# Head denominators as extra columns of the value matmuls, and a new order of casts, splits and SiLUs around the four heads, in a two-layer decoder trunk

## The chip, the cores and the metric

The kernel runs on one core of one Trainium2 chip. The metric is the device time of one execution in microseconds (us). The kernel before takes 823.21 us, the median of three runs (823.09 to 824.32).

A core has these engines, each with its own instruction queue: TensorE (PE, matmuls, with its weight loads shown apart as PEld), VectorE (DVE), ScalarE (ACT), GpSimd (POOL) and SyncE (SP, which issues the loads here).

## The reference

The reference takes 256 tokens of width 1024 through two layers. Layer 0 mixes tokens with a gated MLP, layer 1 with an mLSTM block; each layer goes on with a SwiGLU channel mixer and a gated per-layer embedding, and each residual sum goes through a layer norm. What the change touches is the mLSTM's cell and its output projection. For 256 tokens in two chunks of 128 and a state that starts at zero, a head's cell comes down to this:

```python
s   = (q @ k.T) * d ** -0.5 * exp(dmat - m_t)        # causal, per head; dmat from the gates
num = s @ v                                          # 512 columns of values
den = sum(s, axis=-1)
h   = num / maximum(abs(den), exp(-m_t))
h   = layer_norm(h, norm_g) + skip * xc              # over the head's 512 columns
y   = (h * silu(z)) @ w_out                          # four heads side by side: 2048 features
x   = layer_norm(ALPHA * x + y, ...)
```

The four heads have 512 columns each. `den` is the sum of a row of scores, so it is also `s @ 1`.

## The kernel before, in words

**Precision.** Each matmul of fp32 data is made of three: a value is split into a high and a low part, and high·high, high·low and low·high are added up in PSUM. `split(hi, lo, src)` (lines 150 to 152) is two instructions: a cast on ScalarE writes `hi`, and a subtraction writes `lo`, on VectorE if nothing is said, on GpSimd with `sub=pool`.

**Weights.** All weights stream from DRAM in a fixed list (`weight_plan`). SP loads one piece of 128x1024 (512 KB) at a time into one of four buffers `raw`, at most `LOAD_AHEAD` = 8 pieces ahead of the piece in use. `ahead` (from line 166) also casts and splits up to `CAST_AHEAD` = 4 pieces ahead into one of six buffers `w`: a ScalarE cast and a VectorE subtraction of 128x1024. A `raw` buffer comes free when its subtraction has read it, and only then can SP issue the load that takes its place. The pieces of the output projection are called `mo`, 0 to 15; `pj` and `f` are the first pieces of the channel mixer behind it.

**Order.** A scheduler at build time sets each engine's order from the order in which the code is written and from its own estimates. `issue_after(ops)` holds the instructions in it behind given ones in that order; `behind["cast"]` is such a list for the weights' casts. The engines then run their queues in order and wait on semaphores.

**The mLSTM stage.** It makes the values of each head: `vn[h]` holds 512 high and 512 low columns of each of two token halves. It makes the scores and the gate factors, and per head the weighted scores `sc` (line 910), which are split into `phi` (ScalarE) and `plo` (GpSimd). Then come the four heads. `pv_block(h)` (lines 921 to 963) does this:

- nine matmuls of 512 columns into two PSUM banks `num`, one per token half (lines 930, 931, 934), then six of two columns against a tile of ones into a third bank `pd` (lines 938, 939), which gives the denominators;
- VectorE: the denominator `dn` (944 to 948), statistics of each `num` bank (952, 953), and the scale `rs` and the bias `nb` of the normalization (956, 958, 960), with a power on GpSimd between (957); below, "nb of head h" is the last of these, which the change's text calls the head's norm;
- ScalarE: two instructions of 128x512 that read `num` and write the normalized head `hn` (line 962), after which the banks are free.

Between the heads TensorE makes the last four pieces of `z` (features 12 to 15, bank `zps`, 24 matmuls of 256 columns each), and ScalarE's `z_act` (line 744) writes their SiLU. Four earlier pieces get theirs together in one instruction of 128x1024 (line 916). `h_block(h)` (lines 967 to 981) transposes the head on TensorE (972, bank `tp`) and makes four features on VectorE: `y` = scale and skip (976), `y` times SiLU (977), and a split of `y` into `h`.

**The output projection** multiplies features 0 to 15 with `mo` 0 to 15 into four banks `acc`, two for each token half (lines 238 to 240). PSUM has two pools of four banks, A and B. Heads 0 to 3 take their `num` banks from A in turn, then `acc` does: the first token half's two banks are those that head 2 had, the second half's those of head 3. The first three features are done for the first token half (18 matmuls) and then for the second (18 matmuls), so that the second half's banks are asked for later; features 3 to 15 follow, with the transposes of heads 2 and 3 between them. Behind the projection stands the layer norm of each token half (lines 333 to 342) and the transposes of its result (line 324), on which the channel mixer's matmuls wait.

Of the kernel before, what the change touches and what calls it, by code (L numbers as in the profile page):

```python
# [132 lines left out]
def trunk(ctx, tc, a, out):  # L133
# [35 lines left out]
    def ahead(loads, casts):  # L169
        while at["load"] < min(len(plan), at["use"] + loads):  # L170
            ap = plan[at["load"]][1]
            n = ap.shape[-1]

            t = tl("row" if plan[at["load"]][0] == ("mo", 8) else "raw", [P, n], name="raw")
            for c in HALF if at["load"] < 3 else [slice(0, n)]:
                at["dma"] = sp.dma_start(t[:, c], ap[:, c])
            raws[at["load"]] = t
            at["load"] += 1
        while at["cast"] < min(len(plan), at["use"] + casts):
            i = at["cast"]  # L180
            key, raw = plan[i][0], raws.pop(i)
            n = raw.shape[-1]
            if key in WIDE:
                t = tl("b8", [P, 2, D], F32R, "w")
            else:


                first = ASIDE if stationary(key) and not paired(key) else 0
                step = D + ASIDE if paired(key) else D
                t = tl("w", [P, 2 * D + P], F32R, "w")[:, first:first + 2 * step]  # L190
                t = t.rearrange("p (i n) -> p i n", i=2)[:, :, :D]
            with issue_after(behind["cast"]):
                if key[0] == "bdv":

                    t = t.rearrange("p i n -> p (i n)")[:, :4 * 2 * GW].rearrange("p (j i n) -> p j i n", j=4, i=2)
                    split(t[:, :, 0, :P], t[:, :, 1, :P], raw.rearrange("p (j n) -> p j n", j=4))
                    f = 4 * key[1]
                    pool.tensor_copy(t[:, :, :, P:], wx[:, f:f + 4, :].rearrange("p j (i n) -> p j i n", i=2))
                for c in () if key[0] == "bdv" else HALF if i < 3 else [slice(0, n)]:
                    split(t[:, 0, c], t[:, 1, c], raw[:, c])  # L200
            wt[i] = t
            at["cast"] += 1
# [492 lines left out]
    def mlstm(embed1):  # L695
# [30 lines left out]
        vn = [tl("b8", [P, 2, 2, 512], F32R, "vn") for _ in range(NH)]  # L726
# [16 lines left out]
        def z_act(f, ps):  # L743
            act.activation(sz[f // 8][:, f % 8, :], ps, AF.Silu)

        def z_copy(f, ps):
            act.copy(sz[f // 8][:, f % 8, :], ps)
# [27 lines left out]
        def qv_block(f):  # L775
# [13 lines left out]
            o = tl("cf", [P, 3 * P], name="vsum")[:, :2 * GW].rearrange("p (t n) -> p t n", t=2)  # L789
# [6 lines left out]
            split(vn[h][:, 0, :, c], vn[h][:, 1, :, c], o[:, :, :P], sub=pool)  # L796
# [55 lines left out]
        with tc.manual_schedule(engines={mybir.EngineType.Activation}):  # L852
# [62 lines left out]
            z_copy(*z)  # L915
            act.activation(sz[1][:, 0:4, :], sz[1][:, 0:4, :], AF.Silu)
# [6 lines left out]
        def pv_block(h):  # L923
            hi, lo = ph[h]
            pd = bank("B", [P, 2, 2], "pd")
            num = [bank("A", [P, 512], "num") for _ in range(2)]

            for t, blocks in enumerate(BLOCKS):
                for i, (s, c) in enumerate(blocks):
                    pe.matmul(num[t], hi[:, c], vn[h][:, 0, s, :], start=i == 0, stop=False)  # L930
                    pe.matmul(num[t], hi[:, c], vn[h][:, 1, s, :], start=False, stop=False)
            for t, blocks in enumerate(BLOCKS):
                for i, (s, c) in enumerate(blocks):
                    pe.matmul(num[t], lo[:, c], vn[h][:, 0, s, :], start=False, stop=i == len(blocks) - 1)

            for t, (s, c) in DEN:
                first, end = s == 0, s == t
                pe.matmul(pd[:, t, :], hi[:, c], ones_r[:, :2], start=first, stop=False)
                pe.matmul(pd[:, t, :], lo[:, c], ones_r[:, :2], start=False, stop=end)
# [4 lines left out]
            dve.scalar_tensor_tensor(dn, pd[:, :, 0], -1.0, cols[:, 2:4, h], ALU.mult, ALU.max)  # L944
            dve.tensor_tensor(dn, dn, pd[:, :, 0], ALU.max)
# [3 lines left out]
            st = tl("c", [P, 2, 6], name="hst")  # L949
            mv = tl("c", [P, 2, 2], name="hmv")  # L950
            for t in range(2):
                end = dve.bn_stats(st[:, t, :], num[t])
                dve.bn_aggr(mv[:, t, :], st[:, t, :])
# [6 lines left out]
            dve.scalar_tensor_tensor(nb, mv[:, :, 0], -1.0, rs, ALU.mult, ALU.mult)  # L960
            for t in range(2):
                act.activation(o[:, t, :], num[t], AF.Identity, bias=nb[:, t:t + 1], scale=rs[:, t:t + 1])
            return (end,)

        hs = {}

        def h_block(h):
            for j in range(2):
# [4 lines left out]
                for i in range(2):  # L973
                    f = 4 * h + 2 * j + i
                    y = tl("s", [P, S], name="y")
                    dve.scalar_tensor_tensor(y, tp[:, i, :], par[:, f, 6:7], a1[f // 8][:, f % 8, :], ALU.mult, ALU.add)
                    dve.tensor_tensor(y, y, sz[f // 8][:, f % 8, :], ALU.mult)
                    hs[f] = tl("h", [P, 2, S], F32R, "h")
                    split(hs[f][:, 0, :], hs[f][:, 1, :], y)

        for h in range(NH):
            if h == NH - 1:
                ahead(LOAD_AHEAD, 4)
            end = pv_block(h)
            z_act(*z_mm(12 + h))
            if h == NH - 2:
                h_block(0)
        acc = Down(NI)
        begin = []
        for h in range(NH):  # L990
            if h == 2:
                load_p(1)
            if h + 1 < NH:
                h_block(h + 1)
            for f in range(4 * h, 4 * h + 4):
                if f == 1:

                    behind["cast"] = end
                block = (f, hs.pop(f), weight("mo", f, casts=1 if f >= NI - 2 else None))
                if f < 3:  # L1000

                    begin.append(block)
                    for t in range(2) if f == 2 else ():
                        for b, h2, w in begin:
                            acc.mm(b, t, h2, w)
                else:
# [99 lines left out]
```

## Time and profile before

| | value |
|---|---|
| time, median of 3 runs | 823.21 us (823.09 to 824.32) |
| time of the profiled execution | 823.71 us |
| its span, first to last instruction | 822.0 us |
| TensorE busy | 816.2 us, 99% of the span, 4546 matmuls |
| VectorE busy | 616.9 us, 75% |
| ScalarE busy | 471.8 us, 57% |
| GpSimd busy | 152.1 us, 19% |
| granted TensorE clock | 0.999 of full speed |
| the four heads (first to last matmul against values) | 535.1 to 555 us of the span |
| the output projection, with its layer norm | 559.0 to 613 us |

The profiled execution took 1.7 us more than its span and 0.5 us more than the median. Busy time of a matmul is longer than its place in the queue, since matmuls overlap: what one costs is read from start to start. Rows of the timeline give the start, the length, the engine, the line, the operation and its output and inputs, and, in brackets, how long the engine stood idle before it and what released it.

### The profile page before, as it was taken

What the parts mean: (1) busy time and instruction counts of PE and PEld (TensorE: products, weight loads), DVE (VectorE), ACT (ScalarE), POOL (GpSimd) and SP (SyncE); (2) the same over time, 40 slices, a digit from 0 to 9 for tenths busy, and PEclk for the clock granted to TensorE, in tenths of its full rate; (3) what the DMA queues carried; (4) which work ended last, traced back from release to release, by engine and by line L of the source; (5) the groups of instructions that cost most, each with busy time, mean ns of one, the idle gap of its engine ahead of it and who ended that gap; (6) DMA issues with size and microseconds to landing.
All of it is one profiled execution on the core that took longest, in us unless ns stands there. A gap on an engine that the chain in (4) does not pass through costs nothing.

```text
span 822.0 us, 12471 instructions
## 1 busy us (share of the span) xinstructions
PE 816.2 (99%) x4546; PEld 709.1 (86%) x4546; DVE 616.9 (75%) x985; ACT 471.8 (57%) x824; POOL 152.1 (19%) x209
## 2 busy tenths in 40 slices
PE   9999999999999999999999999999999999999997
PEld 6888888888888888888889999998888888888886
DVE  6667998678966567587878998889896566776674
ACT  6556666565554455465256788776544455665522
POOL 1120643343000000700001677430000000000000
PEclk9999999999999999999999999999999999999999
DMA  8885447558176668667144345453635667886501
GB/s 300 306 306 180 153 156 228 179 182 274 42 258 195 216 217 283 202 228 246 43 151 154 125 164 165 152 199 129 207 126 193 198 206 234 274 256 209 180 1 52
DMA packets 44998, 155.54 MB, mean 189 GB/s; under 512 B 5256, under 2 KB 6024, under 8 KB 44936
## 3 DMA queue, kind: packets, MB, share of 16 engines
q1 hardware_dynamic: 44504, 154.21, 57.2%
q8 instruction: 36, 0.59, 0.3%
q10 hardware_dynamic: 432, 0.52, 0.2%
q14 instruction: 26, 0.21, 0.1%
HBM read 153.67 MB, written 1.05 MB: 188 GB/s over the span
## 4 chain that ended last, share of the span: by engine, by line
PE 98%; DMA 1%; DVE 0%; ACTq 0%; ACT 0%; issue 0%; DVEq 0%
PE acc L238 9%; PE acc L239 9%; PE acc L240 9%; PE pu L258 9%; PE pg L258 9%; PE ups L258 5%; PE pg L262 5%; PE pu L262 5%; PE ups L262 3%; PE vps L240 2%; PE vps L238 2%; PE vps L239 2%; PE xmps L243 2%; PE xmps L244 2%; PE xmps L245 2%; PE gate L287 2%
## 5 line engine op out<-in xcount | busy, mean ns | idle before, releaser
L152 DVE TENSOR_TENSOR w<-raw,w 128x1024 fp32r<-128x1024 f32 (+1 forms) x275 | 333.1, 1219 | 70.1 <-ACT w L152 69.2
L152 ACT CAST w<-raw 128x1024 fp32r<-128x1024 f32 (+1 forms) x275 | 284.9, 1046 | 104.2 <-PE acc L240 23.4
L238 PE MATMUL acc<-w,h 128*128 128x512 f32 x336 | 133.0, 396 | 0.0
L239 PE MATMUL acc<-w,h 128*128 128x512 f32 x336 | 131.3, 391 | 0.0
L240 PE MATMUL acc<-w,h 128*128 128x512 f32 x336 | 131.0, 390 | 0.0
L258 PE MATMUL pu<-xs,w 128*128 128x512 f32 x320 | 79.4, 390 | 0.0
L258 PE MATMUL pg<-xs,w 128*128 128x512 f32 x320 | 79.3, 390 | 0.0
L240 PEld LDWEIGHTS acc<-w,h 128*128 128x128 f32 x336 | 63.1, 188 | 13.8
L238 PEld LDWEIGHTS acc<-w,h 128*128 128x128 f32 x336 | 63.1, 188 | 11.3
L239 PEld LDWEIGHTS acc<-w,h 128*128 128x128 f32 x336 | 63.2, 188 | 11.1
L258 PEld LDWEIGHTS pg<-xs,w 128*128 128x128 f32 x320 | 59.9, 188 | 12.4
L258 PEld LDWEIGHTS pu<-xs,w 128*128 128x128 f32 x320 | 59.8, 188 | 12.3
L269 ACT COPY s<-pg 128x256 f32<-128x256 f32 x40 | 14.9, 372 | 92.1 <-PE pg L262 92.1
L317 POOL TENSOR_TENSOR rs<-ve,mhalf 128x1 f32<-128x1 f32 x8 | 7.6, 954 | 296.7 <-DVE ve L316 251.8
L270 DVE TENSOR_TENSOR s<-s,pg 128x256 f32<-128x256 f32 x40 | 16.8, 420 | 60.7 <-ACT s L269 60.6
L258 PE MATMUL ups<-xs,w 128*128 128x512 f32 x192 | 47.9, 392 | 0.0
L262 PEld LDWEIGHTS pg<-xs,w 128*128 128x128 f32 x320 | 43.2, 188 | 3.4
L262 PE MATMUL pg<-xs,w 128*128 128x256 f32 x320 | 43.9, 280 | 0.0
L262 PE MATMUL pu<-xs,w 128*128 128x256 f32 x320 | 43.8, 279 | 0.0
L258 PEld LDWEIGHTS ups<-xs,w 128*128 128x128 f32 x192 | 35.7, 188 | 7.2
L262 PEld LDWEIGHTS pu<-xs,w 128*128 128x128 f32 x320 | 40.6, 188 | 0.3
L243 PE MATMUL xmps<-xs,w 128*128 128x256 f32 x128 | 36.3, 284 | 0.0
(251 smaller groups left out, 1587.0 us busy)
## 6 DMA issues: line engine op xcount, KB each, us to landing
raw<-in_ffn_d SPq DMA_DIRECT2D x44, 512.0 KB, 4.3
raw<-in_ffn_g SPq DMA_DIRECT2D x40, 512.0 KB, 4.3
raw<-in_ffn_u SPq DMA_DIRECT2D x40, 512.0 KB, 4.1
raw<-in_gm_u SPq DMA_DIRECT2D x24, 512.0 KB, 3.3
raw<-in_gm_wo SPq DMA_DIRECT2D x24, 512.0 KB, 3.3
raw<-in_gm_v SPq DMA_DIRECT2D x21, 512.0 KB, 5.2
raw<-in_ple_gate SPq DMA_DIRECT2D x16, 512.0 KB, 4.5
raw<-in_ml_z SPq DMA_DIRECT2D x16, 512.0 KB, 3.4
```

The costliest lines, as they stand in the source:

```text
L152: return dve.tensor_copy(hi, src) if fast else act.copy(hi, src), sub.tensor_tensor(lo, src, hi.bitcast(F32), ALU.subtract)
L238: pe.matmul(ps, lh, w[:, 0, c], start=start, stop=False)
L239: pe.matmul(ps, ll, w[:, 0, c], start=False, stop=False)
L240: pe.matmul(ps, lh, w[:, 1, c], start=False, stop=stop)
L243: pe.matmul(ps, w[:, 0, c], h, start=start, stop=False)
L244: pe.matmul(ps, w[:, 0, c], l, start=False, stop=False)
L245: pe.matmul(ps, w[:, 1, c], h, start=False, stop=stop)
L258: pe.matmul(ps, w[:, 0, k * P:(k + 1) * P], xs[:, k], start=k == 0, stop=False)
L262: pe.matmul(ps[:, 0], w[:, 1, k * P:(k + 1) * P], xh[:, k, :], start=False, stop=k == KD - 1)
L269: act.copy(o, ps[:, 1])
L270: dve.tensor_tensor(o, o, ps[:, 0], ALU.add)
L287: pe.matmul(ps, xl[:, k, TOK[t]], w[:, 0, c], start=False, stop=k == KD - 1)
```

## The change

- **Values.** `vn[h]` becomes one tile with two views: `vh`, 512 high columns and two columns of ones for each token half, and `vl`, 512 low columns. GpSimd copies the ones once per head. The sum `vsum` moves to another group of buffers.
- **`pv_block`.** The two-column matmuls and the bank `pd` go. A head now takes three banks `num`: `low` from pool A has columns 0 to 255 of both token halves, `top` from A and from B has columns 256 to 511 of one half each and two columns more, the first of which is the denominator. Nine matmuls of 512 columns become eighteen of 256 or 258. The first two operations of `dn` are done per token half (128x1, two of each), the statistics in four instructions of 256 columns instead of two of 512, the normalization in four ScalarE instructions of 128x256 instead of two of 128x512.
- **Casts.** `behind` can hold a list for a single piece. The casts of `mo` 0 to 3 are each held behind an operation on ScalarE and one on VectorE: `mo` 0 behind nb of head 0, `mo` 1 behind nb of head 1, `mo` 2 behind the `y` of feature 1, `mo` 3 behind nb of head 3; later casts stand behind nb of head 3, as before.
- **SiLUs.** The SiLUs of `z` 12 and 13 stand behind the `hn` of head 0, the one of 128x1024 behind the `hn` of head 1 (it stood before that of head 0).
- **Head 0's last feature**, 3, is held back behind nb of head 3, and head 1's transposes move from before the projection's first token half to between the two halves.

On TensorE, the end of head 0's matmuls against the values (`vn` values, `phi` and `plo` scores). Before:

```order
L930 MATMUL num<-vn,phi 128x512
L931 MATMUL num<-vn,phi 128x512
L934 MATMUL num<-vn,plo 128x512 x3
L938 MATMUL pd<-ones_r,phi 128x2
L939 MATMUL pd<-ones_r,plo 128x2
```

Now:

```order
L940 MATMUL num<-vn,phi 128x256
L941 MATMUL num<-vn,phi 128x258
L943 MATMUL num<-vn,phi 128x256 x2
L947 MATMUL num<-vn,plo 128x256
L948 MATMUL num<-vn,plo 128x258
```

The matmuls into `pd` (six per head) are gone; each matmul of 512 columns stands there as two.

On VectorE, head 0's denominators and normalization (`w` from `raw` is the low part of a projection weight, `sc` the weighted scores of a later head). Before:

```order
L910 SCALAR_TENSOR_TENSOR sc<-sc,e 128x384
L944 SCALAR_TENSOR_TENSOR dn<-pd,cols 128x2
L152 TENSOR_TENSOR w<-raw,w 128x1024
L945 TENSOR_TENSOR dn<-dn,pd 128x2
L910 SCALAR_TENSOR_TENSOR sc<-sc,e 128x384
L946 RECIPROCAL dn<-dn 128x2
L948 TENSOR_TENSOR dn_5717<-dn 128x2
L952 BN_STATS hst<-num 128x6 x2
L953 BN_AGGR hmv<-hst 128x2 x2
L956 TENSOR_SCALAR hrs<-hmv,dn_5717 128x1 x2
L958 TENSOR_TENSOR hrs<-hrs,dn 128x2
L960 SCALAR_TENSOR_TENSOR nb<-hmv,hrs 128x2
```

Now:

```order
L956 RECIPROCAL dn<-dn 128x2
L958 TENSOR_TENSOR dn_5725<-dn 128x2
L963 BN_STATS hst<-num 128x6 x3
L916 SCALAR_TENSOR_TENSOR sc<-sc,e 128x384
L964 BN_AGGR hmv<-hst 128x2
L963 BN_STATS hst<-num 128x6
L967 TENSOR_SCALAR hrs<-hmv,dn_5725 128x1
L964 BN_AGGR hmv<-hst 128x2
L967 TENSOR_SCALAR hrs<-hmv,dn_5725 128x1
L969 TENSOR_TENSOR hrs<-hrs,dn 128x2
L971 SCALAR_TENSOR_TENSOR nb<-hmv,hrs 128x2
L152 TENSOR_TENSOR w<-raw,w 128x1024
```

The low parts of the first two projection weights stood before nb of head 0; the first of them now follows it, and there is one behind nb of head 1, one between nb of heads 2 and 3, and the fourth behind nb of head 3.

On ScalarE, the same place (`sz` the gate, `hn` the normalized head). Before:

```order
L744 ACT_TABLE_LOAD
L744 ACTIVATE sz<-zps 128x256
L916 ACTIVATE sz<-sz 128x1024
L962 ACTIVATE hn<-num,nb,hrs 128x512 x2
L152 CAST w<-raw 128x1024
```

Now:

```order
L152 CAST w<-raw 128x1024
L975 ACTIVATE hn<-num,nb,hrs 128x256 x4
L748 ACT_TABLE_LOAD
L748 ACTIVATE sz<-zps 128x256 x2
L152 CAST w<-raw 128x1024
L975 ACTIVATE hn<-num,nb,hrs 128x256 x4
L1015 ACTIVATE sz<-sz 128x1024
```

The table load and the SiLUs moved from ahead of head 0's normalization to behind it, the SiLU of 128x1024 to behind that of head 1.

```diff
-            with issue_after(behind["cast"]):
+            with issue_after(behind.get(key, behind["cast"])):
...
-        vn = [tl("b8", [P, 2, 2, 512], F32R, "vn") for _ in range(NH)]
+        vn = [tl("b8", [P, 2 * D + P], F32R, "vn") for _ in range(NH)]
+        vh = [v[:, :1028].rearrange("p (s n) -> p s n", n=514) for v in vn]
+        vl = [v[:, D + P:].rearrange("p (s n) -> p s n", n=512) for v in vn]
...
-            split(vn[h][:, 0, :, c], vn[h][:, 1, :, c], o[:, :, :P], sub=pool)
+            split(vh[h][:, :, c], vl[h][:, :, c], o[:, :, :P], sub=pool)
+            if j == 3:
+                pool.tensor_copy(vh[h][:, :, 512:], ones_r[:, :4].rearrange("p (s n) -> p s n", s=2))
...
-            z_copy(*z)
-            act.activation(sz[1][:, 0:4, :], sz[1][:, 0:4, :], AF.Silu)
+            behind["hn", -1] = z_copy(*z)
...
-            pd = bank("B", [P, 2, 2], "pd")
-            num = [bank("A", [P, 512], "num") for _ in range(2)]
+            halves = slice(0, 256), slice(256, 512)
+            low = bank("A", [P, 2, 256], "num")
+            top = [bank(w, [P, 258], "num") for w in "AB"]
+
+            den = [n[:, 256:257] for n in top]
+            num = [(low[:, t, :], top[t][:, :256]) for t in range(2)]
 
             for t, blocks in enumerate(BLOCKS):
                 for i, (s, c) in enumerate(blocks):
-                    pe.matmul(num[t], hi[:, c], vn[h][:, 0, s, :], start=i == 0, stop=False)
-                    pe.matmul(num[t], hi[:, c], vn[h][:, 1, s, :], start=False, stop=False)
+
+                    pe.matmul(low[:, t, :], hi[:, c], vh[h][:, s, :256], start=t == i == 0, stop=False)
+                    pe.matmul(top[t], hi[:, c], vh[h][:, s, 256:], start=i == 0, stop=False)
+                    for n, half in zip(num[t], halves):
+                        pe.matmul(n, hi[:, c], vl[h][:, s, half], start=False, stop=False)
             for t, blocks in enumerate(BLOCKS):
                 for i, (s, c) in enumerate(blocks):
-                    pe.matmul(num[t], lo[:, c], vn[h][:, 0, s, :], start=False, stop=i == len(blocks) - 1)
-
-            for t, (s, c) in DEN:
-                first, end = s == 0, s == t
-                pe.matmul(pd[:, t, :], hi[:, c], ones_r[:, :2], start=first, stop=False)
-                pe.matmul(pd[:, t, :], lo[:, c], ones_r[:, :2], start=False, stop=end)
+                    end = i == len(blocks) - 1
+                    pe.matmul(low[:, t, :], lo[:, c], vh[h][:, s, :256], start=False, stop=end and t == 1)
+                    pe.matmul(top[t], lo[:, c], vh[h][:, s, 256:], start=False, stop=end)
...
-            dve.scalar_tensor_tensor(dn, pd[:, :, 0], -1.0, cols[:, 2:4, h], ALU.mult, ALU.max)
-            dve.tensor_tensor(dn, dn, pd[:, :, 0], ALU.max)
+            for t in range(2):
+                dve.scalar_tensor_tensor(dn[:, t:t + 1], den[t], -1.0, cols[:, 2 + t, h:h + 1], ALU.mult, ALU.max)
+                dve.tensor_tensor(dn[:, t:t + 1], dn[:, t:t + 1], den[t], ALU.max)
...
-                end = dve.bn_stats(st[:, t, :], num[t])
-                dve.bn_aggr(mv[:, t, :], st[:, t, :])
+                for i in range(2):
+                    dve.bn_stats(st[:, t, i, :], num[t][i])
+                dve.bn_aggr(mv[:, t, :], st[:, t])
...
-            dve.scalar_tensor_tensor(nb, mv[:, :, 0], -1.0, rs, ALU.mult, ALU.mult)
+            end = dve.scalar_tensor_tensor(nb, mv[:, :, 0], -1.0, rs, ALU.mult, ALU.mult)
+            behind["norm", h] = behind["norm"] = end,
             for t in range(2):
-                act.activation(o[:, t, :], num[t], AF.Identity, bias=nb[:, t:t + 1], scale=rs[:, t:t + 1])
-            return (end,)
+                for n, half in zip(num[t], halves):
+                    behind["hn", h] = act.activation(o[:, t, half], n, AF.Identity, bias=nb[:, t:t + 1], scale=rs[:, t:t + 1])
...
+                    if f == 3:
+                        held.append((f, tp[:, i, :]))
+                    else:
+                        h_feature(f, tp[:, i, :])
...
             if h == NH - 1:
+                behind["mo", 0] = behind["hn", -1], behind["norm", 0][0]
+                behind["mo", 1] = z13, behind["norm", 1][0]
+                behind["mo", 2] = behind["hn", 1], behind["y", 1]
                 ahead(LOAD_AHEAD, 4)
-            end = pv_block(h)
-            z_act(*z_mm(12 + h))
-            if h == NH - 2:
+            pv_block(h)
+            z = z_mm(12 + h)
+            with issue_after((behind["hn", 0],) if h == 0 else ()):
+                z13 = z_act(*z) if h < 2 else z13
+            if h == 2:
+                with issue_after((behind["hn", 1],)):
+                    act.activation(sz[1][:, 0:4, :], sz[1][:, 0:4, :], AF.Silu)
+            if h >= 2:
+                z_act(*z)
+            if h == 2:
                 h_block(0)
+        behind["mo", 3] = behind["hn", 2], behind["norm"][0]
+        with issue_after(behind["norm"]):
+            h_feature(*held.pop())
         acc = Down(NI)
         begin = []
         for h in range(NH):
             if h == 2:
                 load_p(1)
-            if h + 1 < NH:
+            if h == 0:
+                ahead(LOAD_AHEAD, 4)
+            if 0 < h < NH - 1:
                 h_block(h + 1)
             for f in range(4 * h, 4 * h + 4):
                 if f == 1:
-
-                    behind["cast"] = end
+                    behind["cast"] = behind["norm"]
...
                     for t in range(2) if f == 2 else ():
                         for b, h2, w in begin:
                             acc.mm(b, t, h2, w)
+                        if t == 0:
+                            with issue_after(behind["norm"]):
+                                h_block(1)
```

More of the change, by code (lines that the diff above doesn't have):

```diff
@@ L743, in z_act @@
         def z_act(f, ps):
-            act.activation(sz[f // 8][:, f % 8, :], ps, AF.Silu)
+            return act.activation(sz[f // 8][:, f % 8, :], ps, AF.Silu)
         def z_copy(f, ps):
-            act.copy(sz[f // 8][:, f % 8, :], ps)
+            return act.copy(sz[f // 8][:, f % 8, :], ps)
         xms, qs = {}, {}
@@ L788, in qv_block @@
             c = slice(j * P, (j + 1) * P)
-            o = tl("cf", [P, 3 * P], name="vsum")[:, :2 * GW].rearrange("p (t n) -> p t n", t=2)
+            o = tl("m2", [P, 2 * GW], name="vsum").rearrange("p (t n) -> p t n", t=2)
             for t in range(2):
@@ L948, in pv_block @@
             dve.tensor_tensor(dn2, dn, dn, ALU.mult)
-            st = tl("c", [P, 2, 6], name="hst")
+            st = tl("c", [P, 2, 2, 6], name="hst")
             mv = tl("c", [P, 2, 2], name="hmv")
             for t in range(2):
-                end = dve.bn_stats(st[:, t, :], num[t])
-                dve.bn_aggr(mv[:, t, :], st[:, t, :])
+                for i in range(2):
+                    dve.bn_stats(st[:, t, i, :], num[t][i])
+                dve.bn_aggr(mv[:, t, :], st[:, t])
             rs = tl("c", [P, 2], name="hrs")
@@ L959, in pv_block, with h_feature @@
             nb = tl("c", [P, 2], name="nb")
-            dve.scalar_tensor_tensor(nb, mv[:, :, 0], -1.0, rs, ALU.mult, ALU.mult)
+            end = dve.scalar_tensor_tensor(nb, mv[:, :, 0], -1.0, rs, ALU.mult, ALU.mult)
+            behind["norm", h] = behind["norm"] = end,
             for t in range(2):
-                act.activation(o[:, t, :], num[t], AF.Identity, bias=nb[:, t:t + 1], scale=rs[:, t:t + 1])
-            return (end,)
+                for n, half in zip(num[t], halves):
+                    behind["hn", h] = act.activation(o[:, t, half], n, AF.Identity, bias=nb[:, t:t + 1], scale=rs[:, t:t + 1])
         hs = {}
+        def h_feature(f, tp):
+            y = tl("s", [P, S], name="y")
+            behind["y", f] = dve.scalar_tensor_tensor(y, tp, par[:, f, 6:7], a1[f // 8][:, f % 8, :], ALU.mult, ALU.add)
+            dve.tensor_tensor(y, y, sz[f // 8][:, f % 8, :], ALU.mult)
+            hs[f] = tl("h", [P, 2, S], F32R, "h")
+            split(hs[f][:, 0, :], hs[f][:, 1, :], y)
+        held = []
         def h_block(h):
@@ L974, in h_block @@
                     f = 4 * h + 2 * j + i
[L975 to L979, printed above, removed]
+                    if f == 3:
+                        held.append((f, tp[:, i, :]))
+                    else:
+                        h_feature(f, tp[:, i, :])
         for h in range(NH):
             if h == NH - 1:
+                behind["mo", 0] = behind["hn", -1], behind["norm", 0][0]
+                behind["mo", 1] = z13, behind["norm", 1][0]
+                behind["mo", 2] = behind["hn", 1], behind["y", 1]
                 ahead(LOAD_AHEAD, 4)
-            end = pv_block(h)
-            z_act(*z_mm(12 + h))
-            if h == NH - 2:
+            pv_block(h)
[8 more added lines that the diff above has]
+            if h == 2:
                 h_block(0)
+        behind["mo", 3] = behind["hn", 2], behind["norm"][0]
+        with issue_after(behind["norm"]):
+            h_feature(*held.pop())
         acc = Down(NI)
```

## The prediction

> **What bounds the kernel now.** I read the page first, then TensorE's waits, then the timelines around the four heads and around the layer norm behind the projection. The page's busy row, the chain that ended last, and all the waits of TensorE over the whole program:
>
> ```profile
> PE 816.2 (99%) x4546; PEld 709.1 (86%) x4546; DVE 616.9 (75%) x985; ACT 471.8 (57%) x824; POOL 152.1 (19%) x209
> PE 98%; DMA 1%; DVE 0%; ACTq 0%; ACT 0%; issue 0%; DVEq 0%
> PE warm L355 <- PEq L1096: 0.8, 1, 0.8
> PE vps L419 <- ACT xs L375: 0.5, 1, 0.5
> ```
>
> TensorE sets the end and waits nowhere in the heads or in the projection. A microsecond less on TensorE is therefore worth up to a microsecond, but only where nothing else comes to bind in its place; a microsecond on the other engines is worth nothing until it makes TensorE wait.
>
> **What the change takes from TensorE.** Head 0's matmuls against the values, its two-column matmuls, and the `z` piece behind them (start, length):
>
> ```profile
> 535.10 0.39 PE L930 MATMUL num<-vn,phi 128*128 128x512 f32 x1
> ...
> 537.18 0.17 PE L938 MATMUL pd<-ones_r,phi 128*128 128x2 f32 x1
> ...
> 537.76 0.36 PE L243 MATMUL zps<-xs,w 128*128 128x256 f32 x1
> 537.96 0.28 PE L244 MATMUL zps<-xs,w 128*128 128x256 f32 x1
> 538.08 0.28 PE L245 MATMUL zps<-xs,w 128*128 128x256 f32 x1
> ```
>
> The six small matmuls take 537.76 - 537.18 = 0.58 us, and the first matmul behind them holds the queue for 0.20 instead of 0.12: 0.66 per head. The nine of 512 columns take 537.18 - 535.10 = 2.08; eighteen of 256 at 0.12 or a little less take 2.1 to 2.16, some 0.04 more. Left are 0.62 per head and 2.5 us for four: TensorE's ceiling is 823.2 - 2.5 = 820.7 us. Nothing else in the change takes anything from TensorE; the moved transposes stay eight, in another place.
>
> **Where that gain must pass.** From the projection's second token half on, TensorE's work is the same matmuls as before. The end moves as that start moves, unless a later wait is new. The start needs a bank that head 3's normalization has read. VectorE's nb of head 3, ScalarE's normalization, TensorE's first matmul of the second half, then two forms of ScalarE's Identity with scale and bias columns from PSUM, by tile (min/median/max ns):
>
> ```profile
> 561.84 0.15 DVE L960 SCALAR_TENSOR_TENSOR nb<-hmv,hrs 128x2 f32<-128x2 f32 x1
> 562.09 1.45 ACT L962 ACTIVATE hn<-num,nb,hrs 128x512 f32<-128x512 f32 x2 [0.86 <-DVE nb L960]
> 563.20 0.39 PE L238 MATMUL acc<-w,h 128*128 128x512 f32 x1
> L962 ACT ACTIVATE hn<-num,nb,hrs x8: 769/774/780, 545.0 to 562.8; 128x512 f32<-128x512 f32 x8
> L761 ACT ACTIVATE conv<-xmps,par x16: 555/564/567, 444.1 to 514.0; 128x256 f32<-128x256 f32 x16
> ```
>
> Before, the first of two instructions frees the bank, at 562.09 + 0.77 = 562.86; TensorE comes at 563.20, 0.34 later. So TensorE can gain 0.34 us here and no more, unless nb of head 3 comes earlier. Worse, the bank asked for is now `low`, which holds columns of both token halves and is free after the third of four instructions. The pair takes 1.45, so a second starts 0.68 behind the first and 0.10 of each overlaps. At 256 columns a step is 0.56 - 0.10 = 0.46, and the third ends 2 x 0.46 + 0.56 = 1.49 after the first starts. The second half can begin at 562.09 + 1.49 = 563.58 if nb of head 3 stays at 561.84, and s earlier if nb is s earlier. All turns on s.
>
> **When nb of head 3 comes.** First nb of head 0. VectorE's low parts of two projection weights, which the change takes from ahead of it, and GpSimd's last two `plo` and its power for nb:
>
> ```profile
> 536.59 1.23 DVE L152 TENSOR_TENSOR w<-raw,w 128x1024 fp32r<-128x1024 f32 x1
> 539.10 1.21 DVE L152 TENSOR_TENSOR w<-raw,w 128x1024 fp32r<-128x1024 f32 x1
> 539.74 1.45 POOL L152 TENSOR_TENSOR plo<-sc,phi 128x384 fp32r<-128x384 f32 x1 [1.04 <-ACT phi L152]
> 542.22 1.01 POOL L152 TENSOR_TENSOR plo<-sc,phi 128x384 fp32r<-128x384 f32 x1 [1.04 <-ACT phi L152]
> 543.62 0.73 POOL L957 TENSOR_TENSOR hrs<-hrs,mhalf 128x2 f32<-128x2 f32 x1 [0.39 <-DVE hrs L956]
> ```
>
> At most, nb comes earlier by both low parts, 2 x 1.15 = 2.3. At least, by what the power waited behind the last `plo`: 543.62 - 543.23 = 0.4, if the chain of scores, `phi` and `plo` keeps its times. A `plo` beside a low part took 1.45, one alone 1.01; two of them freed of that give 0.9 more. I take 1.3.
>
> [...]
>
> Then the steps from head to head. VectorE's nb of heads 0, 1 and 2 and what stands behind them, and the statistics by tile:
>
> ```profile
> 544.58 0.16 DVE L960 SCALAR_TENSOR_TENSOR nb<-hmv,hrs 128x2 f32<-128x2 f32 x1
> 544.65 0.15 DVE L944 SCALAR_TENSOR_TENSOR dn<-pd,cols 128x2 f32<-128x2 f32 x1
> ...
> 548.07 0.16 DVE L960 SCALAR_TENSOR_TENSOR nb<-hmv,hrs 128x2 f32<-128x2 f32 x1
> 548.15 1.23 DVE L152 TENSOR_TENSOR w<-raw,w 128x1024 fp32r<-128x1024 f32 x1
> 549.30 0.15 DVE L944 SCALAR_TENSOR_TENSOR dn<-pd,cols 128x2 f32<-128x2 f32 x1
> ...
> 554.05 0.15 DVE L960 SCALAR_TENSOR_TENSOR nb<-hmv,hrs 128x2 f32<-128x2 f32 x1
> 554.11 0.75 DVE L977 TENSOR_TENSOR y<-y,sz 128x256 f32<-128x256 f32 x2
> 554.78 0.87 DVE L976 SCALAR_TENSOR_TENSOR y<-tp,par,a 128x256 f32<-128x256 f32 x2
> 555.57 0.41 DVE L977 TENSOR_TENSOR y<-y,sz 128x256 f32<-128x256 f32 x1
> 556.00 1.10 DVE L152 TENSOR_TENSOR h<-y,h 128x256 fp32r<-128x256 f32 x3
> 557.02 0.42 DVE L977 TENSOR_TENSOR y<-y,sz 128x256 f32<-128x256 f32 x1
> L952 DVE BATCH_NORM_STATS2 hst<-num x8: 679/686/694, 541.8 to 559.0; 128x6 f32<-128x512 f32 x8
> ```
>
> Heads 0 to 1 are the bare chain of one head: 548.07 - 544.58 = 3.49. Start to start, a low part costs 549.30 - 548.15 = 1.15, a `y` (555.57 - 554.78) / 2 = 0.40, a product (554.78 - 554.11) / 2 = 0.335, a split of a feature (557.02 - 556.00) / 3 = 0.34. The change lengthens the bare chain. Two more small operations cost 544.65 - 544.58 = 0.07 each. No row has statistics over 256 columns: half of one of 512 (0.60 start to start, its 0.69 less the overlap) would be 0.30, and a `y` of 256 columns from PSUM takes 0.40; I take 0.34, between them and nearer to half because the longer operation is the same one. Four then cost 1.36 against 1.20. Together 0.30 per head (bounds 0.15 and 0.54), the bare chain 3.79.
>
> Now each of the first two steps has one low part: 3.79 + 1.15 = 4.94. The step from head 2 to 3 has one low part and three each of `y`, product and split: 3.79 + 1.15 + 3 x (0.40 + 0.335 + 0.34) = 8.15. The sum is 18.0, before it was 561.84 - 544.58 = 17.26: 0.8 more. With nb of head 0 1.3 earlier, s = 1.3 - 0.8 = 0.5. The second half starts at 563.58 - 0.5 = 563.1, **0.1 earlier** than before, though TensorE alone would be there 2.5 earlier. With the bounds, s lies between 0.4 - 0.8 - 0.7 = -1.1 and 2.3 - 0.8 + 0.45 = 1.95, the start between 1.5 late and 1.6 early.
>
> [...]
>
> The table load and the SiLUs move behind normalizations; ScalarE's 0.86 us of idle before head 3's `hn` covers one cast. If `z` 14's SiLU is late behind the 1.05 us SiLU of 128x1024, TensorE waits for a `top` bank at head 3, but that wait lies inside the one at the second half and isn't added. The ones cost GpSimd four short copies, while the page has it at 19%.
>
> **Behind nb of head 3.** The change leaves VectorE more there. Before nb it had done six `y`, five products and four splits; now three of each. That moves 3 x 0.40 + 2 x 0.335 + 0.34 = 2.2, and a fourth low part, 1.15: 3.35, less s, 2.8 us. What it meets: busy time (PE, PEld, DVE, ACT, POOL) of 562 to 598, VectorE's largest wait there, SP's, and the layer norm's start and end with TensorE's transposes of the second token half:
>
> ```profile
> 562.00:598.00 36.00, 36.00 (x168) 29.96 (x168) 31.98 (x51) 21.34 (x30) 0.00 (x0) 1.00 0.64 205
> DVE h L152 <- ACT h L152: 2.1, 2, 1.6
> SPq L176 <- DVE w L152: 54.9, 20, 13.8
> 596.78 1.23 DVE L152 TENSOR_TENSOR w<-raw,w 128x1024 fp32r<-128x1024 f32 x1 [1.55 <-ACT w L152]
> 598.54 1.37 DVE L333 SCALAR_TENSOR_TENSOR xn<-xn,acc 128x512 f32<-128x512 f32 x2 [0.53 <-PE acc L240]
> 610.22 0.75 DVE L342 SCALAR_TENSOR_TENSOR xn<-xn,rs,row 128x512 f32<-128x512 f32 x1
> 611.74 1.03 PE L324 MATMUL tp<-ident,xn 128*128 128x128 f32 x8
> ```
>
> VectorE has 4.0 us idle in these 36. The 2.1 of waits for ScalarE's `h` can take up added work; the rest is waits for casts, which come with the loads, and SP's loads wait for just these low parts, so a late low part moves its own cover. At 598.54 there are 0.53 more, and behind it VectorE runs without a pause to 610.97, 0.77 before TensorE's transposes. 2.8 - 2.1 - 0.53 = 0.2 late at the layer norm, inside 0.77: **nothing** at the end. If none of the idle took anything up: 2.8 - 0.53 - 0.77 = 1.5 late.
>
> **The sum.** 823.71 of the profiled execution, less 0.1, is 823.6; it lies 0.5 above the median, so 823.1 on the median's scale.
>
> **The rivals.** *The saving comes through.* nb of head 0 comes 2.3 earlier, statistics cost half: the start is 1.6 early, and up to 2.5 if `low` is free sooner still: 821.6 to 820.7, say 821.2. For it speak the two low parts that go from ahead of head 0; against it, that both come back before nb of head 2, and a third before that of head 3. *The layer norm comes late.* s is 0 and no wait but the last takes up the 3.35 us: `pj`'s low part, which stands ahead of the layer norm, ends after 598.0 + 0.53 + 0.77 = 599.3, which is where this begins to decide; 3.35 - 1.3 = 2.0 late, 825.2 us, slower. For it speaks SP's 54.9 us of waiting for low parts; against it the 2.1 us. *The cut matmuls don't cost half:* if those of 258 columns took as long as those of 512, 24 x 0.11 = 2.6 us would eat the saving: no change, 823.2. No row has such a width; the 256 ones speak against it.
>
> **How the numbers follow.** Forecast 823.1 us, chance 0.57, own range by the start's bounds 821.6 to 824.7. The saving comes through: 0.23. The layer norm late: 0.18. Cut matmuls dear: 0.02. About 0.2% (1.6 us) is what a measurement tells from no change: faster 0.23, within it 0.59, slower 0.18. The range 821.0 to 825.2 leaves out about half of each outer case, 0.2 in all.
>
> **What would show it.** TensorE busy falls by some 2.5 us while the span hardly does, and the difference stands as waits of TensorE at 551 to 564 us, for `hn` or nb at the second half. nb of head 0 near 543.3, nb of head 3 near 561.3. Wrong, if TensorE shows no wait there (the saving came through), or if the transposes behind the layer norm start late while the second half's start didn't.

## The result: slower by 0.2%, and the profile after

The changed kernel takes 825.11 us (median of 14 runs, 823.98 to 827.14) beside 823.49 us of the kernel before (median of 14, 823.09 to 824.32) in the runs with which it was compared: a ratio of 1.0020, with an interval of 1.0011 to 1.0028. No change was forecast, at 823.1. The time lies inside the range, but the forecast was no change, and the interval excludes it. The rival "the layer norm comes late" (825.2, slower, chance 0.18) comes closest, though it names only part of the cause.

The profiled execution's span is 823.8 us, 1.8 more than before. The page's busy times and chain, and all the waits of TensorE, of the changed kernel:

```profile
PE 815.7 (99%) x4558; PEld 708.2 (86%) x4558; DVE 617.2 (75%) x1001; ACT 473.7 (58%) x832; POOL 151.3 (18%) x213
PE 27%; DVE 6%; ACT 1%; DMA 1%; issue 1%; POOL 0%; DVEq 0%; ACTq 0%; SPq 0%; POOLq 0%
PE acc L238 <- ACT w L152: 1.1, 1, 1.1
PE warm L355 <- PEq L1135: 0.8, 1, 0.8
PE num L941 <- ACT sz L748: 0.8, 1, 0.8
PE acc L240 <- DVE w L152: 0.5, 1, 0.5
PE acc L238 <- ACT hn L975: 0.4, 1, 0.4
```

The chain of 98% TensorE is gone. TensorE waits at head 3 (0.8, a SiLU), at the second half of the projection (0.4, `hn`), both as the prediction named them, and then twice for a weight: 1.1 and 0.5 us. That weight is `mo` 15, the projection's last, and the prediction has no wait there. One of its signs didn't come: TensorE's busy time fell by 0.5 us (816.2 to 815.7), not by 2.5. Of the 1.3 us that the first wait for `mo` 15 costs from start to start, worked out below, only 1.1 is shown as waiting; so the saving is read from start to start here.

First the heads. The matmuls against the values and the first of the `z` piece behind them (head 0); VectorE's nb of heads 0 to 3; ScalarE's normalization of head 3; the second half's first matmuls:

```profile
535.08 0.28 PE L940 MATMUL num<-vn,phi 128*128 128x256 f32 x1
...
537.23 0.28 PE L243 MATMUL zps<-xs,w 128*128 128x256 f32 x1
537.35 0.28 PE L244 MATMUL zps<-xs,w 128*128 128x256 f32 x1
```

```profile
543.22 0.16 DVE L971 SCALAR_TENSOR_TENSOR nb<-hmv,hrs 128x2 f32<-128x2 f32 x1
548.15 0.16 DVE L971 SCALAR_TENSOR_TENSOR nb<-hmv,hrs 128x2 f32<-128x2 f32 x1
553.18 0.16 DVE L971 SCALAR_TENSOR_TENSOR nb<-hmv,hrs 128x2 f32<-128x2 f32 x1
561.35 0.16 DVE L971 SCALAR_TENSOR_TENSOR nb<-hmv,hrs 128x2 f32<-128x2 f32 x1
561.60 1.93 ACT L975 ACTIVATE hn<-num,nb,hrs 128x256 f32<-128x256 f32 x4 [2.27 <-DVE nb L971]
562.68 0.50 PE L238 MATMUL acc<-w,h 128*128 128x512 f32 x1 [0.38 <-ACT hn L975]
563.01 0.39 PE L239 MATMUL acc<-w,h 128*128 128x512 f32 x1
```

Eighteen matmuls take 537.23 - 535.08 = 2.15, and the one behind them 0.12: 0.59 us saved per head (0.62 forecast). The matmuls of 258 columns stand 0.12 apart like those of 256, so the rival of dear cut matmuls falls. The second half starts at 562.68 instead of 563.20, 0.5 earlier.

Now behind it. The next rows are some of the last loads of weights (SP's queue, `x2` two loads in a row, the length being of the whole group) and the cast of `mo` 15. In the kernel before its low part follows, in the changed kernel TensorE's two waits:

```profile
572.14 4.75 SPq L176 DMA_DIRECT2D raw<-in_ml_wo  x2
583.19 0.33 SPq L176 DMA_DIRECT2D raw<-in_ffn_f  x1
589.67 0.33 SPq L176 DMA_DIRECT2D raw<-in_ml_wo  x1
592.92 1.06 ACT L152 CAST w<-raw 128x1024 fp32r<-128x1024 f32 x1 [2.84 <-DMA raw<-in_ml_wo]
594.01 1.23 DVE L152 TENSOR_TENSOR w<-raw,w 128x1024 fp32r<-128x1024 f32 x1 [0.33 <-ACT w L152]
```

```profile
578.76 1.80 SPq L176 DMA_DIRECT2D raw<-in_ml_wo  x2
590.63 0.33 SPq L176 DMA_DIRECT2D raw<-in_ffn_f  x1
592.10 0.33 SPq L176 DMA_DIRECT2D raw<-in_ml_wo  x1
597.48 1.04 ACT L152 CAST w<-raw 128x1024 fp32r<-128x1024 f32 x1 [0.25 <-DMA raw<-in_ml_wo]
598.58 0.50 PE L238 MATMUL acc<-w,h 128*128 128x512 f32 x1 [1.14 <-ACT w L152]
599.83 0.50 PE L240 MATMUL acc<-w,h 128*128 128x512 f32 x1 [0.53 <-DVE w L152]
```

The pair of loads that SP began at 572.14 begins at 578.76, 6.6 us later. SP catches up most of it, and `mo` 15 (the last of these loads) goes out at 592.10, 2.4 later than before. It then lands more slowly: its cast starts 5.4 us after the issue instead of 3.2. The load of `f` 3 went out 1.5 us ahead of it, where before there were 6.5 us between them (the last section compares this over the runs). So its cast is 4.6 us later, half by the issue and half by the landing. TensorE comes for it at about 597.3 and gets it at 598.58, with its low part at 599.83.

Start to start these two waits cost 2.2 us (597.04 to 598.58 and 598.92 to 599.83, where two matmuls stand 0.23 apart, and about 0.1 more for the first matmul behind each wait: from 598.58 it is 0.34 to the next start). With 0.1 for the restart at 562.68, the account closes: -0.5 + 0.1 + 2.2 = 1.8, and the transposes of the second token half, at 611.74 before, start at 613.58.

What VectorE did meanwhile, in two stretches (busy time of PE, PEld, DVE, ACT, POOL), before and after, and, in the changed kernel, VectorE's last low parts, the layer norm's first and last rows, and TensorE's transposes behind it:

```profile
562.00:580.00 18.00, 18.00 (x85) 14.95 (x85) 17.49 (x31) 12.51 (x19) 0.00 (x0) 1.00 0.54 177
580.00:598.00 18.00, 18.00 (x85) 15.01 (x84) 14.49 (x21) 8.83 (x12) 0.00 (x0) 1.00 0.75 233
```

```profile
562.00:580.00 18.00, 17.62 (x83) 14.51 (x82) 18.00 (x34) 12.33 (x21) 0.00 (x0) 1.00 0.47 150
580.00:598.00 18.00, 17.43 (x81) 14.15 (x79) 13.85 (x22) 8.10 (x11) 0.00 (x0) 1.00 0.70 243
597.26 3.75 DVE L152 TENSOR_TENSOR w<-raw,w 128x1024 fp32r<-128x1024 f32 x3 [2.89 <-ACT w L152]
600.93 1.28 DVE L333 SCALAR_TENSOR_TENSOR xn<-xn,acc 128x512 f32<-128x512 f32 x2
612.52 0.75 DVE L342 SCALAR_TENSOR_TENSOR xn<-xn,rs,row 128x512 f32<-128x512 f32 x1
613.58 1.04 PE L324 MATMUL tp<-ident,xn 128*128 128x128 f32 x8
```

VectorE is idle for 0.5 + 3.5 = 4.0 us before, and for 0 + 4.15 us after. The work that was moved there hardly filled the idle: it came first, pushed the low parts back, and with them the loads, and then VectorE stood 2.9 us at once, waiting for a cast (596.18) that itself waited for the load of `f` 3, which had gone out 7.4 us later than before. The layer norm starts at 600.93, 2.4 late, right behind `pj`'s low part, and ends at 612.52 + 0.75 = 613.27, 2.3 late. TensorE, late by `mo` 15, begins the transposes at 613.58 without waiting: so in this execution `mo` 15 alone set the end, with the layer norm only 0.3 us behind as a second hold. By itself, with the 0.77 us that TensorE had to spare, the layer norm would have cost 1.5.

### The profile page after: what moved, and what is told of

It is laid out like the page before. It is cut to its first block, busy times and chain, and to the rows that moved or that the text cites. A ratio compares the mean times of both kernels' runs of the same rounds, so it can differ in the third digit from the quotient of the medians.

```text
span 823.8 us, 12532 instructions
## 1 busy us (share of the span) xinstructions
PE 815.7 (99%) x4558; PEld 708.2 (86%) x4558; DVE 617.2 (75%) x1001; ACT 473.7 (58%) x832; POOL 151.3 (18%) x213
```

## Experiments

Each was run beside the kernel before on the same chip; the differences below are to that kernel's median there (823.4 us each time; for the changed kernel, +1.6). The changed kernel was not run again beside them, and the intervals are about 0.7 us to each side: differences of 0.6 or 0.7 between two versions are not clear of noise. "Low part" is VectorE's subtraction of 128x1024 for a weight.

**`f` 3 loaded behind `mo` 15.**

```diff
-EARLY |= {("mo", 8 + 2 * k): ("f", 1, k) for k in range(4)}
+EARLY |= {("mo", 15 if k == 3 else 8 + 2 * k): ("f", 1, k) for k in range(4)}
```

> The changed kernel with one load moved: the channel mixer's fourth first piece (f 3) is loaded and cast behind the last projection weight (mo 15) instead of ahead of it. Theory M (the lost time is TensorE's wait for mo 15, whose load is late): the load of mo 15 is issued about 1.5 us earlier, TensorE's two waits of 1.1 and 0.5 us for it go, and about 1.9 us with them: 823.2 us, span 822. Theory L (the recorded rival: pj's low part stands on VectorE ahead of the layer norm and ends too late): three low parts still stand ahead of the layer norm, it starts at 600.9 as before, 825.1 us. Theory B (both, and either is enough): the waits for mo 15 go and the time hardly moves, 824.7 to 825.1, with the wait now in front of the layer norm's transposes.

824.45 us, ratio 1.0013 (1.0004 to 1.0021), +1.1. The waits for `mo` 15 are gone, and the layer norm still starts late:

```profile
599.10 1.22 DVE L152 TENSOR_TENSOR w<-raw,w 128x1024 fp32r<-128x1024 f32 x1 [0.39 <-ACT w L152]
600.25 1.28 DVE L333 SCALAR_TENSOR_TENSOR xn<-xn,acc 128x512 f32<-128x512 f32 x2
612.73 0.52 PE L324 MATMUL tp<-ident,xn 128*128 128x128 f32 x3 [0.69 <-ACT xs L152]
```

The layer norm stands directly behind `pj`'s low part, and TensorE waits 0.7 at the transposes instead. 0.6 of the 1.6 us came back, not clear of noise: between M (1.9) and L (none). The new wait at the transposes is what B expected.

**`pj`'s low part on GpSimd.**

```diff
-                    split(t[:, 0, c], t[:, 1, c], raw[:, c])
+                    split(t[:, 0, c], t[:, 1, c], raw[:, c], sub=pool if key == ("pj", 1, 0) else dve)
```

> The changed kernel with the low part of pj subtracted on GpSimd, which is idle there, instead of VectorE. M: TensorE waits for mo 15 as in the changed kernel, 825.1 us. L: the layer norm starts 1.15 us earlier, 824.0 us. B: it starts about 0.5 us earlier, when mo 15's first column half is done, 824.6 us.

824.34 us, 1.0012 (1.0003 to 1.0021), +1.0. Here the layer norm waits for the accumulators and for nothing else:

```profile
599.29 1.38 DVE L333 SCALAR_TENSOR_TENSOR xn<-xn,acc 128x512 f32<-128x512 f32 x2 [0.59 <-PE acc L240]
```

TensorE's waits for `mo` 15 are 0.2 and 0.5 in this profile, 0.9 less than in the changed kernel, which M didn't expect of an edit that doesn't touch it; its load went out 0.9 earlier. From 558 to 589 us VectorE runs the same instructions in the same order in both. The lead is 0.2 us up to the cast of one earlier weight, which comes 3.8 us after the issue of its load here and 4.5 us in the changed kernel (583.85 and 584.75), and 0.9 from there on. `pj` isn't loaded by then, so no run shows that the edit made this lead. The 0.7 us gained thus don't show what the layer norm's hold costs alone: the other hold was shorter too.

**Both edits.**

> The two edits together: f 3 loaded behind mo 15, and pj's low part on GpSimd. M: as with f 3 moved alone, 823.2 us. L: as with pj alone, 824.0 us. B: both holds are gone and the end moves by clearly more than the sum of what each edit gave alone, 822.7 to 823.2 us.

823.68 us, 1.0004 (0.9995 to 1.0012), +0.3. Neither hold is left, and the loss is nearly gone: both holds together made it. The medians add up (0.6 and 0.7 alone, 1.3 together), which speaks against B, by which one edit alone would give almost nothing. But the single gains lie within the noise, and one of them has the shorter wait for `mo` 15 in it; the changed kernel's own trace, with the holds 0.3 us apart at the end, speaks for B. How the loss divides between M and L stays open.

**The sums of scores as columns, alone.** Casts, SiLUs, feature 3 and head 1's transposes are put back:

```diff
-                behind["mo", 0] = behind["hn", -1], behind["norm", 0][0]
...
-            if h == 2:
-                with issue_after((behind["hn", 1],)):
-                    act.activation(sz[1][:, 0:4, :], sz[1][:, 0:4, :], AF.Silu)
...
-            if 0 < h < NH - 1:
+            if h < NH - 1:
                 h_block(h + 1)
```

> The first half of the change alone: the sums of scores as columns of the values, with the halved matmuls, statistics and normalizations; casts, SiLUs, head 0's last feature and head 1's transposes where they were before. If the loss comes from the moved casts and features alone (M, L, B), TensorE finds its weights in time and this is not slower than before: 823.2 or less. If the longer normalization chain costs by itself (0.3 us per head and 0.7 for the third quarter, 0.3 of it covered), nb of head 3 is about 1.2 us later than before, TensorE waits at the second half's start for 1.6 us more, and it is 824.8 us.

824.54 us, 1.0013 (1.0004 to 1.0022), +1.2: the second reading. TensorE's longest wait, at the second half, and nb of head 3:

```profile
PE acc L238 <- ACT hn L976: 0.9, 1, 0.9
```

```profile
563.08 0.15 DVE L972 SCALAR_TENSOR_TENSOR nb<-hmv,hrs 128x2 f32<-128x2 f32 x1
```

nb of head 3 is 1.2 later than before (561.84), as expected, but 0.4 of that is there already when the heads start (535.54 instead of 535.10); the longer chain costs about 0.8 in this profile. No saving of TensorE comes through it, and TensorE waits for no weight.

**The new order alone.** Values, denominators and normalization as before, with `pd` and 512 columns; casts, SiLUs and features in the new places.

> The second half of the change alone: values, denominators and normalization as before (two-column matmuls, 512 columns), with the new places of casts, SiLUs, head 0's last feature and head 1's transposes. C: VectorE is as crowded behind nb of head 3 as in the changed kernel, less 1.2 us because the chain of each head is 0.3 shorter, and TensorE is 0.5 us later at mo 15: its waits are 0.5 to 1 us shorter, the end 0.5 to 1.3 us later than in the kernel before, 823.9 to 824.7. If the loss needs the longer chain of the new normalization, no wait for weights is left and it is 823.4 or less.

823.60 us, 1.0002 (0.9994 to 1.0011), +0.2: less than C expected (C: VectorE has too much work behind nb of head 3, so that low parts and loads come late), and TensorE waits for no weight. Its one wait here is for the layer norm; nb of heads 0 to 3 follow:

```profile
PE tp L324 <- DVE xn L342: 0.3, 1, 0.3
542.84 0.16 DVE L961 SCALAR_TENSOR_TENSOR nb<-hmv,hrs 128x2 f32<-128x2 f32 x1
547.48 0.16 DVE L961 SCALAR_TENSOR_TENSOR nb<-hmv,hrs 128x2 f32<-128x2 f32 x1
552.14 0.16 DVE L961 SCALAR_TENSOR_TENSOR nb<-hmv,hrs 128x2 f32<-128x2 f32 x1
559.99 0.16 DVE L961 SCALAR_TENSOR_TENSOR nb<-hmv,hrs 128x2 f32<-128x2 f32 x1
```

Its steps are 4.64, 4.66 and 7.85; those of the changed kernel 4.93, 5.03 and 8.17. The changed normalization costs about 0.3 us of VectorE per head, and nb of head 3 is 1.4 later with it, 0.3 of which the heads start later (535.08 instead of 534.80). The new order alone has just room for what it moves, as the wait of 0.3 shows; for this 1.1 us more it has none.

**The new order, with 0.335 us more on VectorE per head.** This is the direct test of the last sentence:

```diff
                 dve.bn_stats(st[:, t, :], num[t])
+                if t == 1:
+                    dve.bn_stats(tl("c", [P, 6], name="more"), num[t][:, :256])
                 dve.bn_aggr(mv[:, t, :], st[:, t, :])
```

> The kernel with only the new order of casts and features (normalization as before), and in each head one more statistic of 128x256 that nothing reads: 0.335 us more on VectorE per head, about what the changed normalization adds. TensorE has the same work as in the kernel with only the new order, 823.6 us. Theory C: nb of head 3 comes about 1.2 us later, at 561.2 as in the changed kernel; everything on VectorE behind it is that much later, mo 15 is late and the layer norm starts late: 824.6 to 825.5 us. If the loss needs the cut matmuls or their banks: 823.6 us.

824.83 us, 1.0016 (1.0007 to 1.0025), +1.4. nb of head 3 comes at 560.97, and TensorE waits for `mo` 15 again, with TensorE's own work unchanged:

```profile
560.97 0.16 DVE L963 SCALAR_TENSOR_TENSOR nb<-hmv,hrs 128x2 f32<-128x2 f32 x1
PE acc L240 <- DVE w L152: 0.5, 1, 0.5
PE acc L238 <- ACT w L152: 0.2, 1, 0.2
```

1.0 us later on VectorE made the median 1.2 us higher (0.6 between the two profiled executions). The load of `mo` 15 goes out at 591.2 in both; what is later is its landing, 5.3 us from issue to cast instead of 4.1, with the load of `f` 3 1.1 us ahead of it instead of 1.8. The layer norm starts 0.4 later. The scheduler put one `y` ahead of nb of head 2 in this kernel, so the order isn't quite the same; the work is.

**Five low parts on GpSimd,** those of `f` 0 to 3 and `pj`, in the changed kernel.

```diff
-                    split(t[:, 0, c], t[:, 1, c], raw[:, c])
+                    split(t[:, 0, c], t[:, 1, c], raw[:, c], sub=pool if key in ON_POOL else dve)
```

> The changed kernel with no load moved, but the low parts of the channel mixer's first five pieces (f 0 to 3 and pj), which stand among those of the projection weights, subtracted on GpSimd instead of VectorE. Theory C (crowding: VectorE has too much behind nb of head 3, so low parts, and the loads that wait for their buffers, come late): 5 x 1.15 = 5.8 us leave VectorE, mo 15 is there in time, the layer norm starts when the accumulators are done, and left of TensorE's 2.5 us is what the waits in the heads (0.8 and 0.4, 0.2 more for two restarts) leave: 1.1 us under the kernel before, 822.3. Theory D (mo 15 lands late because its load goes out in a burst with those of f 3 and pj): these loads are not earlier, a subtraction on GpSimd even holds its buffer for 2.4 us instead of 1.2; TensorE waits for mo 15 as in the changed kernel, 824.5 us or more.

825.44 us, 1.0025 (1.0016 to 1.0035), +2.0: C's time is missed by 3 us, though `mo` 15 is in time. GpSimd's first of these subtractions; two products of VectorE behind it; a cast of ScalarE for a weight; and TensorE's wait for the casts behind it:

```profile
571.11 3.63 POOL L153 TENSOR_TENSOR w<-raw,w 128x1024 fp32r<-128x1024 f32 x1 [10.01 <-ACT w L153]
573.19 2.17 DVE L983 TENSOR_TENSOR y<-y,sz 128x256 f32<-128x256 f32 x2
603.80 1.06 ACT L153 CAST w<-raw 128x1024 fp32r<-128x1024 f32 x1 [4.44 <-DMA raw<-in_ffn_g]
610.12 0.50 PE L285 MATMUL first<-w,xs 128*128 128x512 f32 x1 [1.81 <-ACT xs L153]
```

Two products that take 0.75 elsewhere take 2.17 beside GpSimd's subtraction: VectorE loses 1.4 us to it where it was to save 1.15. The buffers are held longer (GpSimd's subtractions take 2.4 to 3.6 us, VectorE's 1.2), the load of the next weight is late, ScalarE stands 4.4 us before its cast (603.80, where the changed kernel has 599.92), and the casts for the layer norm queue behind. So this run doesn't tell C from D.

**The same edit in the kernel before.**

> The same edit in the kernel before, as a control. C: TensorE waits for no weight there, so there is nothing to gain: 823.4 us. If taking low parts from VectorE gains by itself, whatever the change did, it is faster by about as much as in the changed kernel, 822 us or less.

823.40 us, 1.0001 (0.9992 to 1.0010): nothing to gain there, as expected, and nothing lost.

**All that, and the low parts of `mo` 0 to 2 on GpSimd,** with the SiLU of 128x1024 one head later.

> The edit of f_pool, and with it the low parts of mo 0 to 2 on GpSimd too, and the SiLU of 128x1024 behind head 2's normalization instead of head 1's. If the steps between the nb's are the sum of what stands on VectorE between them, nb of head 3 comes about 3 us earlier than in the changed kernel, TensorE waits neither at head 3 nor at the second half, and all of its 2.5 us is seen: 820.9 us. [...]

828.81 us, 1.0067 (1.0054 to 1.0079), +5.4. GpSimd's first low part, and an operation of VectorE on two columns on the way to nb of head 0:

```profile
542.81 2.39 POOL L153 TENSOR_TENSOR w<-raw,w 128x1024 fp32r<-128x1024 f32 x1
542.88 2.34 DVE L970 TENSOR_TENSOR hrs<-hrs,dn 128x2 f32<-128x2 f32 x1 [1.46 <-POOL hrs L969]
```

0.16 us of work takes 2.34, the whole length of GpSimd's subtraction. nb of head 0 comes 2.0 later than in the changed kernel instead of earlier.

**Four subtractions left out, without GpSimd.** ScalarE copies the high parts of `f` 0 to 3 once more, in the place of the low parts.

```diff
-                    split(t[:, 0, c], t[:, 1, c], raw[:, c])
+                    if key in ON_ACT:
+                        act.copy(t[:, 0, c], raw[:, c])
+                        act.copy(t[:, 1, c], raw[:, c])
+                    else:
+                        split(t[:, 0, c], t[:, 1, c], raw[:, c])
```

> The changed kernel without the four subtractions of f 0 to 3 on VectorE: ScalarE copies these pieces' high parts a second time instead, so it leaves the low parts of these four weights out (1.05 us each on ScalarE, and no engine but VectorE and ScalarE touched). [...] Theory D (mo 15's load goes out in a burst with f 3's and pj's, whatever VectorE does): the wait for mo 15 stays, 824.5 us or more.

823.22 us, 0.9997 (0.9989 to 1.0006), -0.2: D falls, by which the wait stays whatever VectorE does (`mo` 15's load still goes out 0.9 behind that of `f` 3). C, by which 4.6 us less on VectorE bring low parts and loads earlier and `mo` 15 in time, stands, though the time is 0.9 above the 822.3 us that I expected of it. The edit also frees these four buffers without VectorE, so it shows the whole chain through the buffers, and not VectorE's load apart from it. The load of `mo` 15 and the start of the layer norm, which now waits 2.9 us for the accumulators:

```profile
585.12 0.33 SPq L177 DMA_DIRECT2D raw<-in_ml_wo  x1
597.95 1.37 DVE L338 SCALAR_TENSOR_TENSOR xn<-xn,acc 128x512 f32<-128x512 f32 x2 [2.89 <-PE acc L245]
```

The load goes out 7.0 us earlier than in the changed kernel, and TensorE's only waits left are those in the heads, 0.8 and 0.3. What stays is the 0.5 us by which the second half starts earlier. My 822.3 took only the named waits off TensorE's 2.5; it should have gone by the second half's start, which nb of head 3 sets and which this edit doesn't move.

No version was clearly faster than the kernel before. The bound that is left even with the crowding taken away is the time of nb of head 3, and taking work on VectorE ahead of it to GpSimd made it later in the one run that tried (563.94 instead of 561.35).

## Why the prediction was wrong, step by step

- **TensorE's saving**: 0.62 per head forecast, 0.59 measured. Right.
- **The statistics at 256 columns**: 0.34 start to start forecast; three in a row took 1.01 us to the next start, 0.335 each. Per head 0.30 more on VectorE forecast; the steps of the run with the new order alone and of the changed kernel differ by 0.29, 0.37 and 0.32. Right. Four statistics cost 4 x 0.335 - 1.20 = 0.14 more than two of 512 (0.16 forecast), since neighbours overlap: one lasts 0.42 (median of 16), and the next starts 0.335 behind it.
- **nb of head 0 and of head 3**: 543.3 and 561.3 forecast, 543.22 and 561.35 measured. Right, and the choice of 1.3 between 0.4 and 2.3 with it: the `plo` that took 1.53 and 1.45 before took 1.01 and 1.02, with no low part beside them.
- **The bank behind the third of four normalizations**: wrong, by 0.4 us to the good. The four start 0.455 apart from 561.60, so the second ends at 562.62 and the third at 563.07; TensorE started at 562.68. So it waited for the second, which points to `top`'s bank as the one asked for first. The second half started at 562.68, not at 563.1.
- **"2.8 - 2.1 - 0.53 = 0.2 late at the layer norm ... nothing at the end"**: this is the step that failed. It let VectorE's idle take up 2.1 + 0.53 = 2.6 us of the work added behind nb of head 3. The 2.8 us was about right: from nb of head 3 to the layer norm VectorE worked 35.19 us instead of 31.99, 3.2 more, begun 0.5 earlier. But its idle in that stretch only fell from 4.56 to 4.23, so it took up 0.3, and the layer norm came 2.4 late. The prediction had this case too ("if none of the idle took anything up ... 1.5 late"), and 1.5 is what the layer norm's end would have cost by itself. The idle stands behind waits that the added work moves along: low part late, buffer late, load late, cast late, low part late. The prediction says this of the idle that hangs on loads, and took it for 1.9 of the 4.0 us only. The other 2.1, waits for ScalarE's `h`, became 1.3, and in their place came the 2.9 us ahead of the low parts of `f` 3, `mo` 15 and `pj`.
- **Where it is paid**: the prediction looked for it in front of the layer norm, by `pj`'s low part, with the point of decision at 599.3. It ended near 600.9, so the rival's condition was met. But in the changed kernel's trace TensorE paid at `mo` 15, which the text doesn't have, and the layer norm was the hold right behind it; the loss went nearly whole only when both were lifted. Before, `mo` 15's low part ended at 595.2, and TensorE came for it at 598.1: 2.9 us to spare, 2.4 with the earlier start. Its load went out 2.4 us later, which would just have used that up; the slower landing made the loss. The chance of 0.18 for this case was too low for work on an engine that was busy for 17.49 of the 18 us behind it. That the time came out so near the rival's 825.2 is in part luck, since the rival has no wait for `mo` 15. Of the two signs of being wrong, the second came: the transposes behind the layer norm started late (613.58), and the second half didn't.

What the runs leave open: why one load took 3.8 us to its cast with `pj` on GpSimd and 4.5 in the changed kernel, how the loss divides between the two holds, and how much of the landing time of 5.4 us is due to the neighbouring loads.

## What to carry to other kernels

Idle time of a busy engine can be counted on to cover added work only if what ends that idle doesn't itself depend on the engine's earlier work. Where loads wait for buffers that the engine frees, the idle can move back with the work: here 0.3 us of 4.56 was taken up, and 2.4 of the delay of 2.8 arrived. So look, for every weight in the stretch, at the time between its last preparation and its first use, not only at the next stage. And a saving on the bounding engine is worth what the next wait on its path leaves: here 2.4 us of TensorE became 0.5.

## What the runs showed that I had not expected

An operation of VectorE on two columns, 0.16 us long, took 2.34 beside a subtraction of GpSimd of 2.39, and two products 2.17 instead of 0.75. The short operation ended at 545.22, 0.02 behind GpSimd's subtraction (545.20). The price shows in the run with five low parts on GpSimd: moving one of 1.15 us cost VectorE 1.4 us there. It isn't paid beside every operation: beside `pj`'s low part on GpSimd, the layer norm's first two operations, which read PSUM, took 1.38 us, and 1.37 before.

The load of `mo` 15, 512 KB, took 3.2 us from issue to cast before, and 3.4 in the run with the columns alone, where the load ahead of it went out about 6.5 us earlier; it took 3.9 to 4.7 where 1.8 or 1.9 us lay between them (the new order alone, and the two runs with `f` 3 behind), and 5.2 to 5.4 at 1.5 us or less (the changed kernel, `pj` on GpSimd alone, the new order with the statistic). That a late load that catches up in a burst lands later still is what these runs suggest; none moved this distance alone.
